# RMSNorm with every row written twice: two tiles' copies moved to VectorE as wide instructions, one copy and its store moved behind a row of the next tile

## The chip, the cores and the metric

The kernel runs on one core of one Trainium2 chip. The metric is the device time of one execution in microseconds (us), as the median of several runs. A ratio is the mean time of one kernel's runs over that of the other's in the same rounds, so it is not quite the ratio of the medians quoted. Beside each experiment the kernel before ran on the same chip; its medians there lie between 239.42 and 239.53 us.

## The reference

```python
def reference(x, gamma):                 # x: 8 x 512 x 2048 float32
    x_rep = np.repeat(x, 2, axis=1)      # every row twice
    rms = np.sqrt((x_rep ** 2).mean(axis=-1, keepdims=True) + 1e-6)
    return ((x_rep / rms) * gamma[None, None, :]).astype(np.float32)
```

33.6 MB are read and, as each row is written twice, 67.1 MB written.

## The kernel before

A tile is 512 rows: 4 rows (K) in each of 128 partitions. Its buffer has 8 row slots. A load fills slots 4 to 7; the scaled row k goes to slot 2k and a copy of it to slot 2k+1, so that a store writes 64 KB per partition in one piece. There are 8 tiles and 3 buffers. Cuts are marked with `# ...`.

```python
def store(i, k0, k1):
    nc.sync.dma_start(out=out_t[i, :, R * k0 * D : R * k1 * D],
                      in_=ys[i][:, R * k0 : R * k1, :].rearrange("p j d -> p (j d)"))
# ... square(i, k): ScalarE square with a row sum, then a root -> rms
# ... scale(i, k, rms): VectorE reciprocal, then row * rstd * gamma into slot 2k
def repeat(i, k0, k1, copy):
    y_r = ys[i].rearrange("p (k r) d -> p k r d", r=R)
    copy(out=y_r[:, k0:k1, 1, :], in_=y_r[:, k0:k1, 0, :])

def compute(i):
    for k in range(K):
        scale(i, k, square(i, k))
    repeat(i, 0, K // 2, nc.scalar.copy)            # first half: ScalarE
    repeat(i, K // 2, K, nc.vector.tensor_copy)     # second half: VectorE
# ... load(0), gamma, load(1), load(2)
loads_after = {2: (3, 4, 5), 4: (6, 7)}
for i in range(ntiles):
    compute(i)
    store(i, 0, K)
    for j in loads_after.get(i, ()):
        load(j, nc.sync)
```

All loads and stores are issued by SyncE, in program order. A load waits for the store that last used its buffer. In the queue the transfers stand as: loads 0, 1, 2, stores 0, 1, 2, loads 3, 4, 5, stores 3, 4, loads 6, 7, stores 5, 6, 7. There are five **turnovers**, places where loads give way to stores or stores to loads: in front of store 0, load 3, store 3, load 6 and store 5.

Of the kernel before, what the change touches and what calls it, by code (L numbers as in the profile page):

```python
# [1 line left out]

# [4 lines left out]


@with_exitstack
def kernel(  # L10
    ctx: ExitStack,
    tc: tile.TileContext,
    x: bass.AP,
    gamma: bass.AP,
    out: bass.AP,
):
    nc = tc.nc
    P = nc.NUM_PARTITIONS
    f32 = mybir.dt.float32
    Act = mybir.ActivationFunctionType  # L20
    Alu = mybir.AluOpType

    B, S, D = x.shape
    Bo, So, Do = out.shape
    R = So // S
    assert R == 2 and D == Do and B == Bo and So == S * R
    eps = 1e-6
    inv_d = 1.0 / float(D)


    K = 4
    N = B * S
    assert N % (P * K) == 0
    ntiles = N // (P * K)
    x_t = x.rearrange("b s d -> (b s) d").rearrange("(n p k) d -> n p k d", p=P, k=K)
    out_t = out.rearrange("b s d -> (b s) d").rearrange("(n p j) d -> n p (j d)", p=P, j=K * R)

    singles = ctx.enter_context(tc.tile_pool(name="singles", bufs=1))
    rows = ctx.enter_context(tc.tile_pool(name="rows", bufs=3))
    junk = ctx.enter_context(tc.tile_pool(name="junk", bufs=1, space=bass.MemoryType.PSUM))  # L40
    small = ctx.enter_context(tc.tile_pool(name="small", bufs=8))

    ys = []

    def load(i, eng, parts=1):


        y = rows.tile([P, K * R, D], f32, name="y")
        step = K // parts
        for k in range(0, K, step):  # L50
            at = K * (R - 1) + k
            eng.dma_start(out=y[:, at : at + step, :], in_=x_t[i, :, k : k + step, :])
        ys.append(y)

    def store(i, k0, k1):
        nc.sync.dma_start(  # L56
            out=out_t[i, :, R * k0 * D : R * k1 * D],
            in_=ys[i][:, R * k0 : R * k1, :].rearrange("p j d -> p (j d)"),
        )

    def square(i, k):
        sq = junk.tile([P, D], f32, name="sq")
        ss = small.tile([P, 1], f32, name="ss")
        nc.scalar.activation(  # L64
            out=sq[:], in_=ys[i][:, K * (R - 1) + k, :], func=Act.Square, accum_out=ss[:]
        )
        rms = small.tile([P, 1], f32, name="rms")
        nc.scalar.activation(out=rms[:], in_=ss[:], func=Act.Sqrt, scale=inv_d, bias=eps_t[:])  # L68
        return rms

    def scale(i, k, rms):
        rstd = small.tile([P, 1], f32, name="rstd")
        nc.vector.reciprocal(out=rstd[:], in_=rms[:])  # L73
        nc.vector.scalar_tensor_tensor(  # L74
            out=ys[i][:, R * k, :], in0=ys[i][:, K * (R - 1) + k, :], scalar=rstd[:], in1=gamma_b[:],
            op0=Alu.mult, op1=Alu.mult,
        )

    def repeat(i, k0, k1, copy):
        y_r = ys[i].rearrange("p (k r) d -> p k r d", r=R)  # L80
        copy(out=y_r[:, k0:k1, 1, :], in_=y_r[:, k0:k1, 0, :])  # L81

    def compute(i):
        for k in range(K):
            scale(i, k, square(i, k))
        repeat(i, 0, K // 2, nc.scalar.copy)
        repeat(i, K // 2, K, nc.vector.tensor_copy)


    ctx.enter_context(tc.manual_schedule())  # L90
    load(0, nc.sync, parts=2)
    gamma_b = singles.tile([P, D], f32, name="gamma_b")
    cuts = [0, *range(D // 4, D + 1, D // 8)]
    for c0, c1 in zip(cuts, cuts[1:]):
        nc.scalar.dma_start(out=gamma_b[0:1, c0:c1], in_=gamma[c0:c1].partition_broadcast(1))  # L95
    nc.gpsimd.partition_broadcast(out_ap=gamma_b[:], in_ap=gamma_b[0:1, :])  # L96
    eps_t = singles.tile([P, 1], f32, name="eps_t")
    nc.vector.memset(eps_t, eps)  # L98
    load(1, nc.sync)
    load(2, nc.sync)  # L100



    assert ntiles == 8
    loads_after = {2: (3, 4, 5), 4: (6, 7)}
    for i in range(ntiles):
        compute(i)
        store(i, 0, K)
        for j in loads_after.get(i, ()):
            load(j, nc.sync)  # L110


# [1 line left out]
_INS = ['x', 'gamma']  # L114
_OUTS = [((8, 1024, 2048), 'float32')]


# [23 lines left out]
```

## Time and profile before

| | before |
|---|---|
| median, 6 runs (lowest to highest) | 239.53 us (239.31 to 239.66) |
| VectorE, ScalarE busy | 96.5 and 101.0 us of 237.9 |
| share of the DMA engines' time that the one queue takes | 98.5% |
| rate from 2 to 235.5 us | 430 GB/s |
| stores 0, 3 and 5 issued at | 27.05, 115.86, 160.08 us |
| their first data at | 32.4, 119.4, 177.4 us |

The prediction below shows the lines.

### The profile page before, as it was taken

What the parts mean: (1) busy time and instruction counts of PE and PEld (TensorE: products, weight loads), DVE (VectorE), ACT (ScalarE), POOL (GpSimd) and SP (SyncE); (2) the same over time, 40 slices, a digit from 0 to 9 for tenths busy, and PEclk for the clock granted to TensorE, in tenths of its full rate; (3) what the DMA queues carried; (4) which work ended last, traced back from release to release, by engine and by line L of the source; (5) the groups of instructions that cost most, each with busy time, mean ns of one, the idle gap of its engine ahead of it and who ended that gap; (6) DMA issues with size and microseconds to landing.
All of it is one profiled execution on the core that took longest, in us unless ns stands there. A gap on an engine that the chain in (4) does not pass through costs nothing.

```text
span 237.9 us, 287 instructions
## 1 busy us (share of the span) xinstructions
DVE 96.5 (41%) x73; ACT 101.0 (42%) x106; POOL 2.5 (1%) x5
## 2 busy tenths in 40 slices
DVE  0049999960000000059999960000199990000000
ACT  2697999900000000099999920000599960000000
POOL 0030000000000000000000000000000000000000
DMA  7999998989899998999998999989998989999994
GB/s 265 436 446 441 441 441 353 530 353 496 386 452 430 397 485 353 441 441 441 441 518 364 464 419 430 452 369 430 435 518 364 518 364 485 397 452 430 408 474 176
DMA packets 2464, 100.69 MB, mean 423 GB/s; under 512 B 279, under 2 KB 285, under 8 KB 286
## 3 DMA queue, kind: packets, MB, share of 16 engines
q1 hardware_dynamic: 2448, 100.66, 98.5%
q14 instruction: 2, 0.02, 0.0%
q10 hardware_dynamic: 14, 0.01, 0.0%
HBM read 33.56 MB, written 67.11 MB: 423 GB/s over the span
## 4 chain that ended last, share of the span: by engine, by line
DMA 58%; ACT 12%; DVE 9%; issue 1%; POOLq 1%; ACTq 1%; SPq 0%
DMA y<-in_x_dram 33%; DMA out_dram<-y 21%; ACT sq L64 8%; DVE y L74 7%; DMA gamma_b<-in_gamma_dram 4%; ACT y L81 3%; DVE y L81 2%; ACT rms L68 1%; POOLq L136 1%; ACTq L95 1%; DVE rstd L73 0%; POOLq L96 0%; SPq L56 0%
## 5 line engine op out<-in xcount | busy, mean ns | idle before, releaser
L64 ACT ACTIVATE sq<-y 128x2048 f32<-128x2048 f32 x32 | 59.7, 1865 | 87.8 <-DMA y<-in_x_dram 87.8
L74 DVE SCALAR_TENSOR_TENSOR y<-y,rstd,gamma_b 128x2048 f32<-128x2048 f32 x32 | 75.3, 2352 | 4.1 <-POOL gamma_b L96 3.0
L73 DVE RECIPROCAL rstd<-rms 128x1 f32<-128x1 f32 x32 | 5.0, 158 | 94.6 <-ACT rms L68 94.3
L81 ACT COPY y<-y 128x4096 f32<-128x4096 f32 x8 | 28.7, 3590 | 1.4 <-DVE y L74 1.4
L81 DVE COPY y<-y 128x4096 f32<-128x4096 f32 x8 | 18.3, 2294 | 0.3
L68 ACT ACTIVATE rms<-ss,eps_t 128x1 f32<-128x1 f32 x32 | 9.4, 295 | 1.0
L64 ACT ACTIVATION_READ_ACCUMULATOR sq<-y 128x1 f32 x32 | 6.0, 187 | 0.0
L64 ACT ACT_TABLE_LOAD x1 | 1.3, 1283 | 3.0 <-issue 3.0
L96 POOL PARTITION_BROADCAST gamma_b<-gamma_b x1 | 2.3, 2294 | 12.2 <-DMA y<-in_x_dram 12.2
L68 ACT ACT_TABLE_LOAD x1 | 1.3, 1283 | 0.0
L98 DVE MEMSET eps_t<- 128x1 f32 x1 | 0.1, 59 | 0.8 <-PEq L125 0.8
L125 POOL MEMSET const-uint8-127<- 128x1 uint8 x1 | 0.1, 102 | 0.0
L125 POOL MEMSET const-bfloat16-1.0<- 128x1 bf16 x1 | 0.1, 101 | 0.0
L125 POOL MEMSET const-float32-0.0<- 128x1 f32 x1 | 0.1, 98 | 0.2 <-issue 0.2
L125 POOL MEMSET const-float32-1.0<- 128x1 f32 x1 | 0.1, 98 | 0.0
## 6 DMA issues: line engine op xcount, KB each, us to landing
y<-in_x_dram SPq DMA_DIRECT2D x7, 4096.0 KB, 14.6
y<-in_x_dram SPq DMA_DIRECT2D x2, 2048.0 KB, 7.4
out_dram<-y SPq DMA_DIRECT2D x8, 24.4
gamma_b<-in_gamma_dram ACTq DMA_DIRECT2D x6, 1.0 KB
gamma_b<-in_gamma_dram ACTq DMA_DIRECT2D x1, 2.0 KB
```

The source lines that it names most:

```text
L64: nc.scalar.activation(out=sq[:], in_=ys[i][:, K * (R - 1) + k, :], func=Act.Square, accum_out=ss[:])
L68: nc.scalar.activation(out=rms[:], in_=ss[:], func=Act.Sqrt, scale=inv_d, bias=eps_t[:])
L73: nc.vector.reciprocal(out=rstd[:], in_=rms[:])
L74: nc.vector.scalar_tensor_tensor(out=ys[i][:, R * k, :], in0=ys[i][:, K * (R - 1) + k, :], scalar=rstd[:], in1=gamma_b[:], op0=Alu.mult, o ...
L81: copy(out=y_r[:, k0:k1, 1, :], in_=y_r[:, k0:k1, 0, :])
L95: nc.scalar.dma_start(out=gamma_b[0:1, c0:c1], in_=gamma[c0:c1].partition_broadcast(1))
L96: nc.gpsimd.partition_broadcast(out_ap=gamma_b[:], in_ap=gamma_b[0:1, :])
L98: nc.vector.memset(eps_t, eps)
L125: nc = _bacc.Bacc("TRN2", target_bir_lowering=False, num_devices=1)
L136: with _tile.TileContext(nc) as tc:
```

## The change

In tiles 0 and 3 it frees ScalarE of its half of the copy; VectorE copies the whole tile there with one wide instruction. It also lets ScalarE start tile 6's first square before it copies tile 5's first half; store 5 must then wait for that copy.

```diff
     def compute(i):
         for k in range(K):
-            scale(i, k, square(i, k))
-        repeat(i, 0, K // 2, nc.scalar.copy)
-        repeat(i, K // 2, K, nc.vector.tensor_copy)
+            rms = square(i, k)
+            if i == 6 and k == 0:
+                repeat(5, 0, K // 2, nc.scalar.copy)
+                store(5, 0, K)
+            scale(i, k, rms)
+        if i in (0, 3):
+            repeat(i, 0, K, nc.vector.tensor_copy)
+        else:
+            if i != 5:
+                repeat(i, 0, K // 2, nc.scalar.copy)
+            repeat(i, K // 2, K, nc.vector.tensor_copy)
 ...
-        store(i, 0, K)
+        if i != 5:
+            store(i, 0, K)
```

## The prediction

> **What bounds the kernel now.** I began with the page: what each engine is busy with, then the strip of 40 slices and the table of DMA queues.
>
> ```profile
> DVE 96.5 (41%) x73; ACT 101.0 (42%) x106; POOL 2.5 (1%) x5
> ...
> DMA  7999998989899998999998999989998989999994
> ...
> q1 hardware_dynamic: 2448, 100.66, 98.5%
> ```
>
> VectorE and ScalarE work for two fifths of the span. The queue that SyncE issues on keeps the 16 DMA engines at 98.5% of the 237.9 us, and no inner slice falls below 8 tenths. Every load and store is on that queue. So I asked for the busy time of 2 to 235.5 us in one window, to see whether any hole is hidden by rounding.
>
> ```profile
> 2.00:235.50 233.50, 96.48 (x72) 101.02 (x106) 2.29 (x1) 1.00 1.00 430
> ```
>
> The last two columns are the DMA share and the rate: 1.00 and 430 GB/s. The bytes are fixed (33.56 MB read, 67.11 MB written), and 100.66 MB / 430 GB/s = 234.1 us; with about 1.7 us before the first packet and 2 us after the last that is the span. **The transfers are the bound.** A change of copies can matter only if it leaves the transfers without work for a while, or changes their order or size.
>
> So the question is how late each store may be issued. The chain of waits has the issues; its long DMA pieces are mostly waiting in line, since a store alone moves 8.39 MB, which at 430 GB/s is 19.5 us.
>
> ```profile
> 24.69 2.30 DVE y L81
> ...
> 27.05 25.77 DMA out_dram<-y
> 52.84 48.32 DMA y<-in_x_dram
> ...
> 115.86 24.36 DMA out_dram<-y
> 140.24 29.08 DMA y<-in_x_dram
> ```
>
> Read: store 0 is issued at 27.05 as soon as VectorE's copy ends, and lands 25.77 us later, not 19.5. Store 3 is issued at 115.86 and lands after 24.36. Each stood in line behind loads for some 5 us. To see when a store's own data begins I cut narrow windows around those moments. The window counts a packet at its start, and the packet records of the trace show 32 KB packets for loads and 64 KB for stores, one per partition. Columns: window, length, VectorE, ScalarE, GpSimd, clock, DMA share, GB/s.
>
> ```profile
> 31.00:32.30 1.30, 1.26 (x3) 1.27 (x4) 0.00 (x0) 1.00 0.00 0
> 32.30:32.60 0.30, 0.30 (x1) 0.30 (x1) 0.00 (x0) 1.00 3.02 1306
> ```
>
> ```profile
> 119.00:119.40 0.40, 0.40 (x1) 0.40 (x1) 0.00 (x0) 1.00 0.00 0
> 119.40:119.80 0.40, 0.40 (x1) 0.40 (x1) 0.00 (x0) 1.00 3.80 1638
> ```
>
> ```profile
> 177.30:177.80 0.50, 0.50 (x1) 0.50 (x1) 0.00 (x0) 1.00 2.00 852
> ```
>
> The zeros are no idle time: the last load packets are still moving. By the packet records the first 64 KB packets of store 0 start between 32.4 and 33.0 us, of store 3 between 119.4 and 120.1, of store 5 between 177.4 and 178.8, each directly behind the load in front of it. The **lead** (issue to first data) is 5.4 us for store 0 and 3.5 us for store 3. Store 5 is issued at 160.08, right behind load 7, and has 17.3 us. What lead is needed? The first load is issued at 0.72 us and its packets begin at 1.73 us, on the last engines by about 2.5: 1.0 to 1.8 us from an idle queue.
>
> **What the Trainium skill says.** "DMA: Bandwidth & Descriptors", section Queues, rings and completion order: on each DMA engine the descriptors of a queue are consumed in ring order. The trace agrees: the loads' packets finish before a store's begin at all three places. "HBM Reference", section Access, says that a core streaming alone reaches about 425 GB/s; the trace has 430. "VectorE: DVE Perf Modes", section The perf-mode tier table: an fp32 copy within SBUF runs at two elements a cycle (1227 ns for 2048). The trace's 128x4096 copy at 2294 ns agrees: 4096 / 2 / 0.96 GHz is 2133 ns, and the other 160 ns I take as a fixed cost of each instruction.
>
> **The change part by part.**
>
> ```profile
> L81 ACT COPY y<-y 128x4096 f32<-128x4096 f32 x8 | 28.7, 3590 | 1.4 <-DVE y L74 1.4
> L81 DVE COPY y<-y 128x4096 f32<-128x4096 f32 x8 | 18.3, 2294 | 0.3
> ```
>
> Tiles 0 and 3. Removed: two ScalarE copies, 2 x 3.59 = 7.2 us of an engine that is 42% busy. Widened: two VectorE copies from 128x4096 to 128x8192. I take the same two elements a cycle, as the pattern still has an even outer dimension (4 rows) and no overlap of source and destination: 8192 / 2 / 0.96 = 4267 ns, + 160 = 4.43 us, so **+2.13 us** on each.
> - Store 0: 27.05 + 2.13 = 29.18 us, lead 32.4 - 29.2 = 3.2 us. Needed 1.0 to 1.8. Hidden.
> - Store 3: 115.86 + 2.13 = 117.99, lead 119.4 - 118.0 = 1.4 us on the first engine and 2.1 on the last. Needed 1.0 to 1.8. Hidden, but this is the tight place: at worst some engines wait about 0.4 us.
>
> VectorE carries the 2.13 us into tiles 1, 2, 4 and 5, because it is nearly unbroken within a group. Store 1 would go from 39.2 to 41.3 us, store 2 from 51.39 to 53.5; they are wanted at 51.7 and 71.0, each a store (19.3 us) behind the one before. Store 4 goes from 128.25 to 130.4, wanted at 138.7. All have 8 us or more. Load 3, issued at 52.84 behind store 2, goes to about 53.9 and is wanted at 90. ScalarE starts tile 1 about a microsecond sooner; nothing waits for that.
>
> Tile 5 and 6. The copy of tile 5's first half (3.59 us) leaves 134.84 us and goes behind row 0's square of tile 6. Load 6 releases that square at 169.34, the root ends at 171.67, the copy ends near 171.6 + 3.6 = 175.2. So store 5 is issued at **175.2 instead of 160.08**, 15.1 us later. Lead: 177.4 - 175.2 = 2.2 us. Needed 1.0 to 1.8. Hidden. Its place in line is the same: loads 6 and 7 stood ahead of it already, and no other transfer overtakes.
> ScalarE's later squares of tile 6 move by 3.6 us, VectorE's by about 3.4 (its row 0 is not delayed). Store 6: 184.0 + 3.4 = 187.4, wanted at 196.7. Store 7: 196.4 + 3.4 = 199.8, wanted at 216.0. Hidden.
>
> Sum on the path: 0 + 0 + 0, with 0 to 0.4 us at store 3. Central 0.1 us: 239.63 + 0.1, called **239.7 us**.
>
> **The rivals.**
> - A store comes too late and the DMA engines run dry, at store 3 first. The lead left of 1.4 us is close to the 1.0 to 1.8 needed. If a store needs a lead of 2 us, the hole is 0.6 us there and nothing at store 5, so 240.2. If it needs 3 us, holes of 1.6 and 0.8 us: 242. Against it: I know no case of such need in this trace; the shortest lead it has is 3.5 us, and that left no hole.
> - The wide copy loses its fast mode. Then 8192 / 0.96 + 160 = 8.7 us, +6.4 over before: store 0 at 33.5 and store 3 at 122.2, holes of about 2.1 to 2.9 and 3.8 to 4.6 us, 246 us in all. Against it: the 4096 copy has the same kind of pattern, rows 4096 elements apart, and runs at the fast rate.
> - It gets faster. The last load packets before store 0 (starts 30.3 to 30.9) took about 2.1 us where 1.21 is the rule, on all engines: some 0.9 us lost, of unknown cause. If it comes from the moment of store 0's issue, the new moment may change it, so -0.9 to +0.9. Apart from that the transfers have no hole to close, and 2% (4.8 us) is not to be found.
> - VectorE becomes the bound: its sum goes to about 100.8 us of 238. It doesn't.
>
> **Range and chances.** The three runs of before lie within 0.15 us. The range takes the stretched packets away at its lower end (-0.7) and a hole of 1 us at its upper end: 238.9 to 240.6. Slower by 2% would need the lost fast mode, or several holes: 0.02. Faster by 2%: 0.01. Within: 0.97.
>
> **What the profile of the changed kernel would show.** Two VectorE copies of 128x8192 at 4.43 us and six of 128x4096; ScalarE's copies down to six. The store issues at 29.2, 118.0 and 175.2 us. The first data of stores 0, 3 and 5 still at 32.4, 119.4 and 177.4 (less 0.9 on all if the stretch vanishes), and a DMA share of 1.00 between 2 and 235.5 us. The prediction is wrong if store data begins visibly later than the end of the load in front of it, at store 3 above all, or if the order of transfers differs.

## The result and the profile after

| | before | after |
|---|---|---|
| median, 6 runs each | 239.53 us | 239.82 us |
| lowest to highest | 239.31 to 239.66 | 239.13 to 240.31 |
| ratio, 95% interval | | 1.0011 (0.9992 to 1.0029) |
| VectorE, ScalarE busy | 96.5, 101.0 us | 100.7, 94.3 us |

The time is the same. The page of the changed kernel (busy time by engine, the DMA strip, the queue), then its window from 2 to 235.5 us:

```profile
DVE 100.7 (42%) x73; ACT 94.3 (40%) x104; POOL 2.5 (1%) x5
...
DMA  7999999899998989999999989899999999898984
...
q1 hardware_dynamic: 2448, 100.66, 98.2%
```

```profile
2.00:235.50 233.50, 100.66 (x72) 94.34 (x104) 2.29 (x1) 1.00 1.00 430
```

4.2 us of work came to VectorE and 6.7 us left ScalarE, and the last two columns of the window are what they were: the DMA engines full, 430 GB/s. The groups of copies (busy us, mean ns of one, idle time in front):

```profile
L81 ACT COPY y<-y 128x4096 f32<-128x4096 f32 x6 | 21.6, 3594 | 5.2 <-DVE y L74 5.2
L81 DVE COPY y<-y 128x4096 f32<-128x4096 f32 (+1 forms) x8 | 22.6, 2826 | 0.3
```

ScalarE has six copies left. The second line's 2826 ns is a mean over two shapes. The timeline has the wide one by itself, in tiles 0 and 3, with SyncE's issues (SPq) behind it; the third piece has ScalarE's late copy of tile 5 and the issue of store 5. Columns: start, length, engine, line. A line with x2 or x3 takes several issues together: its start is that of the first, its length reaches to the end of the last.

```profile
24.48 4.43 DVE L81 COPY y<-y 128x8192 f32<-128x8192 f32 x1
...
28.93 12.56 SPq L56 DMA_DIRECT2D out_dram<-y  x2
```

```profile
113.01 4.43 DVE L81 COPY y<-y 128x8192 f32<-128x8192 f32 x1
...
117.47 0.34 SPq L56 DMA_DIRECT2D out_dram<-y  x1
```

```profile
171.31 3.59 ACT L81 COPY y<-y 128x4096 f32<-128x4096 f32 x1
...
174.92 25.06 SPq L56 DMA_DIRECT2D out_dram<-y  x3
```

So store 0 is issued 1.9 us later than before, store 3 1.6 and store 5 14.8. Did their data come later? The same narrow windows as in the prediction, of the changed kernel (last columns: DMA share, GB/s; packets are counted at their start):

```profile
31.00:31.50 0.50, 0.47 (x3) 0.47 (x3) 0.00 (x0) 1.00 0.00 0
31.50:32.30 0.80, 0.80 (x1) 0.18 (x1) 0.00 (x0) 1.00 3.04 1312
```

```profile
119.00:119.40 0.40, 0.40 (x1) 0.34 (x2) 0.00 (x0) 1.00 2.65 1147
...
177.30:177.80 0.50, 0.47 (x2) 0.50 (x1) 0.00 (x0) 1.00 3.89 1638
```

They came no later. 1312 GB/s over 0.8 us is 1.05 MB, the first 64 KB packet of store 0 on each of 16 engines; they start from 31.5 us on, where before it was 32.4. Store 3's start from 118.9 (before 119.4), store 5's from 177.3 (177.4). But store 0's data is 0.85 us *earlier*, although it was issued later, and at the end of the kernel nothing is left of that. The trace lists every DMA packet with its start, length and size. By these packet records of the two traces, this is what the last packet before each turnover took beyond the rule (1.213 us for a load's 32 KB, 2.418 for a store's 64 KB), as a mean over the 16 engines:

| us lost in front of | store 0 | load 3 | store 3 | load 6 | store 5 | sum |
|---|---|---|---|---|---|---|
| before | 0.87 | 0.00 | 0.03 | 0.02 | 0.04 | 0.96 |
| after | 0.10 | 0.35 | 0.00 | 0.24 | 0.15 | 0.84 |

The loss at the turnovers moved from one place to others. In the profiled run of the changed kernel one engine ran on to 237.33 us where the slowest of before stopped at 236.76: it lost 0.8 us in front of store 5, and up to 1.1 are lost on one engine in front of load 6.

### The profile page after: what moved, and what is told of

Its sections match the earlier page's. It is cut to its first block, busy times and chain, and to the rows that moved or that the text cites. A ratio compares the mean times of both kernels' runs of the same rounds, so it can differ in the third digit from the quotient of the medians.

```text
span 238.5 us, 285 instructions
## 1 busy us (share of the span) xinstructions
DVE 100.7 (42%) x73; ACT 94.3 (40%) x104; POOL 2.5 (1%) x5
## 3 DMA queue, kind: packets, MB, share of 16 engines
q1 hardware_dynamic: 2448, 100.66, 98.2%
## 4 chain that ended last, share of the span: by engine, by line
DMA 45%; DVE 22%; ACT 8%; issue 6%; POOLq 1%; ACTq 1%; SPq 0%
DMA y<-in_x_dram 32%; DVE y L74 19%; DMA out_dram<-y 9%; ACT sq L64 5%; DMA gamma_b<-in_gamma_dram 4%; ACT y L81 3%; DVE y L81 3%; POOLq L147 1%; DVE rstd L73 1%; ACTq L105 1%; ACT rms L68 1%; SPq L56 0%; POOLq L106 0%; SPq L52 0%
## 5 line engine op out<-in xcount | busy, mean ns | idle before, releaser
L81 ACT COPY y<-y 128x4096 f32<-128x4096 f32 x6 | 21.6, 3594 | 5.2 <-DVE y L74 5.2
L81 DVE COPY y<-y 128x4096 f32<-128x4096 f32 (+1 forms) x8 | 22.6, 2826 | 0.3
```

## The experiments

Two theories stand against each other. **Theory:** the DMA engines are the bound, each store has a lead from issue to first data, and a later issue costs nothing until the lead falls under what a transfer needs from issue to first data, and from there on one for one. **Rivals:** the two parts cost and gain and cancel; the queue makes good a late issue later on; the copies themselves are on the path. The diffs are against the changed kernel unless "before" is named.

### Each part alone

`a1_wide_only`: the wide copies, tile 5 as before.

```diff
-            if i == 6 and k == 0: ...copy and store of tile 5...
-            if i != 5:
-                repeat(i, 0, K // 2, nc.scalar.copy)
+            repeat(i, 0, K // 2, nc.scalar.copy)
 ...
-        if i != 5:
-            store(i, 0, K)
+        store(i, 0, K)
```

> Part one of the change alone: tiles 0 and 3 wide, tile 5 as before. My theory (the 16 DMA engines are the bound and each store has a lead left) expects the time of before, 239.6 us within 0.6, with stores 0 and 3 issued near 28.9 and 117.5 us and their data directly behind the load in front. Rival (two costs and gains of the two parts cancel in the whole change): this one alone is off by over 1 us, and the tile 5 part alone is off by as much the other way.

Measured: 239.81 us (239.51 to 241.42, 6 runs), ratio 1.0033 (1.0006 to 1.0061). Stores 0 and 3 issued at 28.93 and 117.47 us.

`a2_late5_only`: tile 5's copy and store moved, no wide copy.

```diff
-        if i in (0, 3):
-            repeat(i, 0, K, nc.vector.tensor_copy)
-        else:
+        if True:
```

> Part two of the change alone: tile 5's first half copied behind row 0 of tile 6, its store issued near 175 us instead of 160. Theory: 239.6 us within 0.6, because the store's data could not begin before 177.3 us in either case. Rival (cancelling parts): off by over 1 us against the first part.

Measured: 239.49 us (239.31 to 239.59), ratio 0.9998 (0.9986 to 1.0010). Store 5 was issued at 175.13 us and its data began at 177.36, as in the kernel before.

Both parts are worth nothing by themselves, so no cancelling is needed. The wide copies' 0.3% is barely clear of noise and comes from two of the six runs, above 241 us; the other four have a mean of 239.68. The two were not profiled, so what they had is not known. The section on turnovers takes up the profiled run (239.84 us).

### How late is too late

`b1_row1` and `b3_row3`: tile 5's copy behind row 1 or row 3 of tile 6 instead of row 0.

```diff
-            if i == 6 and k == 0:
+            if i == 6 and k == 1:      # b3_row3: k == 3
```

> The changed kernel, but tile 5's copy behind row 1's square of tile 6 (one square, accumulator read and root later, 2.22 us). Store 5 is then issued near 177.1 us. Theory: the store needs 1.0 to 1.8 us from issue to first data, so it begins at 178.2 to 178.9 where the load in front ended at 177.3 to 178.3: a hole of about 0.7 us on the engines that end last, 240.3 to 240.6 us in all, and 240 to 241 allowing for noise. Rival (the queue makes good a late issue, or the lead is not needed at all): 239.6 us, no hole. Rival (a store needs a lead of over 2.4 us): hole of 2 us or more, 241.5.

> The same copy behind row 3's square of tile 6: store 5 issued near 181.6 us, 6.7 us later than in the changed kernel. Theory: past the lead every microsecond counts in full, so the hole is about 6.7 - 1.4 = 5.3 us on the engines that end first and 5.0 on the last, and the time 244.6 us within 0.7. Rival (a later stretch makes it good, since store 6 and 7 have leads of 9 us and more): under 241 us.

Measured: 238.82 us (238.78 to 239.42; ratio 0.9976, 0.9963 to 0.9989) for row 1, 243.42 us (243.33 to 244.07; ratio 1.017) for row 3. The first is a miss, and not only in size: later was a little faster. The second came out 0.5 us under my range. SyncE's timeline of b1_row1, then that of b3_row3 and its windows (there is a hole when no packet starts for longer than one takes):

```profile
176.68 22.84 SPq L56 DMA_DIRECT2D out_dram<-y  x3
```

```profile
181.93 18.40 SPq L56 DMA_DIRECT2D out_dram<-y  x3
```

```profile
178.80:180.00 1.20, 1.17 (x3) 1.20 (x1) 0.00 (x0) 1.00 0.00 0
180.00:182.70 2.70, 2.67 (x2) 2.70 (x2) 0.00 (x0) 1.00 0.00 0
182.70:183.00 0.30, 0.30 (x1) 0.30 (x1) 0.00 (x0) 1.00 8.18 3495
```

The loads had ended by 178.74 us, the store is issued at 181.93, its first data starts at 182.77 on the first and 182.91 on the last engine (3495 GB/s x 0.3 us is one 64 KB packet on all 16). **So a store into an idle queue needed 0.84 to 0.98 us from issue to first data.** In b1_row1 store 5 is issued at 176.68 and starts at 177.52: the same 0.84. The last engine's load ended at 177.84, so the hole was on the early engines only (13 of 16), and those were not the ones that end last. Between the two profiled runs, 244.07 - 238.82 = 5.25 us, and store 5's data starts 5.07 to 5.25 us later: past the lead it counts in full, though stores 6 and 7 still had leads of 17 and 22 us. (The profiled run of b3_row3 was its slowest by 0.65 us; the medians differ by 4.60.)

`c1_t3_again` and `c4_t3_again`: the same at store 3, with one row, or all four, of tile 3 copied a second time.

```diff
             repeat(i, 0, K, nc.vector.tensor_copy)
+            if i == 3:
+                repeat(i, 0, 1, nc.vector.tensor_copy)      # c4_t3_again: 0, 4
```

> The changed kernel with one row of tile 3 (128x2048) copied a second time behind the wide copy, so that store 3 is issued 1.2 us later, near 118.7 us, while the load in front of it ends at 118.9 on the first DMA engine and 119.7 on the last. The two runs with store 5 held back showed 0.84 to 0.98 us from issue to first data. Theory (a store's hole counts only as far as it passes the engine that ends last): data at 119.5 to 119.7, no loss, 239.6 us within 0.6. Rival (the hole on the first engine counts): 0.7 us more, 240.4.

> The changed kernel with the whole wide copy of tile 3 done twice: store 3 issued 4.43 us later, near 121.9 us. Theory: data at 122.7 to 122.9, 3.1 us behind the engine that ends last, so 242.6 us within 0.7. It is also what the change would have cost there if the wide copy had run at one element a cycle. Rival (the place matters, since three tiles of work are behind it to make it good): under 240.5.

Measured: 240.60 us (240.49 to 240.77; ratio 1.0046) and 243.96 us (243.92 to 244.07; ratio 1.0185). Both are misses, by 0.4 and 0.7 us beyond my ranges. SyncE's timeline and the windows of c4_t3_again:

```profile
121.74 0.34 SPq L56 DMA_DIRECT2D out_dram<-y  x1
```

```profile
120.80:122.50 1.70, 1.67 (x3) 0.00 (x0) 0.00 (x0) 1.00 0.00 0
122.50:122.80 0.30, 0.30 (x1) 0.00 (x0) 0.00 (x0) 1.00 8.19 3495
```

Again 0.84 to 0.99 us from issue to data, at another place. Between the two kernels the time differs by 3.36 us and store 3's first data (119.16 in c1, 122.58 in c4) by 3.42. The hole itself is therefore as the theory has it. What both have on top came later: c1 has no hole in front of store 3 that the last engine feels (its loads end at 119.25, the store starts at 119.30), but the last packets in front of load 6 took 0.61 us too long and those in front of store 5 0.73. So c1's 240.60 us lies nearer to the 240.4 that I had given to the rival, a hole that counts on the first engine, than to my theory. What speaks against the rival is the trace, where the loss stands at other places, and b1_row1, where a hole on the early engines cost nothing. Whether c1's late store 3 brought the later losses about is not shown.

### Are the copies on the path at all?

`d_all_wide`: all tiles wide on VectorE, none on ScalarE (against before).

```diff
-        repeat(i, 0, K // 2, nc.scalar.copy)
-        repeat(i, K // 2, K, nc.vector.tensor_copy)
+        repeat(i, 0, K, nc.vector.tensor_copy)
```

> The kernel before with every tile's copy as one wide VectorE instruction and none on ScalarE. Theory: all stores keep a lead (store 0 and 3 as in the changed kernel, 4 near 131.8 us where 138.2 is wanted, 6 and 7 over 9 us), VectorE 112 us busy of 238, so 239.6 us within 0.6. Rival (VectorE, which gets all copies, becomes the bound of a stage): over 241.

Measured: 239.89 us (239.46 to 240.34), ratio 1.0014 (1.0001 to 1.0027). VectorE is busy for 113.3 us and ScalarE for 73.4, and the time is the same within 0.3%.

`e_no_copy` and its control `e2_copy_rows` (against before): each store becomes two of 8 KB rows. The first has no copies and reads slot 2k for both output rows; the control keeps the copies and reads slot 2k+1 for the odd rows.

```diff
-        nc.sync.dma_start(...one store of 64 KB per partition...)
+        for r in range(R):
+            nc.sync.dma_start(
+                out=out_t[i].rearrange("p (k r d) -> p k r d", r=R, d=D)[:, k0:k1, r, :],
+                in_=ys[i].rearrange("p (k r) d -> p k r d", r=R)[:, k0:k1, 0, :])   # control: r for 0
```

> The kernel before without any copy: each store is two of 4.19 MB, both reading the scaled rows, one writing the even and one the odd output rows. The result is right. Packets of 8 KB take the place of 64 KB. Theory: taking all 47 us of copies away gains nothing; the load packets show 0.611 us for 16 KB and 1.213 for 32 KB, so little cost per packet, and the time is 239.0 to 241. Rival (the copies are a cost): under 238.5.

> The control for the kernel without copies: the same two stores of 8 KB rows, but the copies of before kept and the odd rows read from them. Theory: the same time as without copies within 0.6 us. Rival: over 1 us longer than without copies.

Measured: 243.04 us (242.87 to 243.43) without copies and 242.77 (242.52 to 242.97) with them, ratios 1.0150 and 1.0141. The page of e_no_copy, then of e2_copy_rows (engines, queue):

```profile
DVE 78.4 (32%) x65; ACT 73.4 (30%) x98; POOL 2.5 (1%) x5
...
q1 hardware_dynamic: 9744, 100.66, 99.1%
```

```profile
DVE 96.5 (40%) x73; ACT 101.0 (42%) x106; POOL 2.5 (1%) x5
...
q1 hardware_dynamic: 9744, 100.66, 99.3%
```

45.7 us of engine work less (18.1 of VectorE, 27.6 of ScalarE), and not a microsecond of time. Both are slower than the kernel before, and e_no_copy lies 2.0 us above my range: the same bytes go in 9744 packets instead of 2448. By the packet records one of 8 KB takes 0.309 us, so eight take 54 ns more than one of 64 KB (2.418); for the 64 of those that each engine has, that is 3.5 us, about what is measured. With the packets alike, removing every copy gains nothing: that is the cleanest form of the answer.

### Why later was sometimes faster: the turnovers

In b1_row1 store 5 came just at the end of the load and the whole was faster. First theory: a store that waits in the queue stretches the last load packets in front of it, whatever the kernel. `f_row1_narrow` is a2_late5_only with row 1.

```diff
-            if i == 6 and k == 0:       # of a2_late5_only
+            if i == 6 and k == 1:
```

> The kernel before with only tile 5's copy moved, behind row 1 of tile 6 instead of row 0. The changed kernel in that form came out at 238.82 us, 0.24% under before, against my expectation. New theory: a store queued well ahead stretches the last load packets in front of it, and a store that comes just at their end does not; then the narrow form gains as well, 238.9 us within 0.3. Rival (the gain needs the wide copies too, or was chance): 239.5 us.

Measured: 239.48 us (239.35 to 239.62), ratio 0.9997. A miss by 0.3 us, where the rival had 239.5; the theory in that form fell. In the narrow kernel the packets in front of store 5 were not stretched to begin with (0.01 us with row 0, 0.00 with row 1), so there was nothing to win.

`h_wide_row1`: tiles all wide, except tile 5, whose copy is behind row 1 of tile 6.

```diff
-            if i == 6 and k == 0:
+            if i == 6 and k == 1:
-        if i in (0, 3):
+        if i != 5:
```

> The kernel with all copies wide (239.89 us; the last load packets in front of store 5 took 0.6 us too long on average) but tile 5's copy split as in the changed kernel and placed behind row 1 of tile 6, so that store 5 comes just at the end of the load. Theory (in the wide kernels a store queued ahead stretches the load in front of it, one just in time does not): 239.2 us within 0.3. Rival (the gain of that placing with two wide tiles was chance): 239.9 us.

Measured: 238.90 us (238.78 to 238.94), ratio 0.9979 (0.9966 to 0.9991), where all-wide had 239.89. (It differs from all-wide in tile 5's split copy too; b1_row1 differs from the changed kernel in the row alone.) So the gain with wide copies was no chance. The windows show what is odd in it. First a1_wide_only, where store 5 is issued at 159.38 us; then b1_row1, where it is issued 17 us later, at 176.68:

```profile
177.30:177.90 0.60, 0.60 (x1) 0.57 (x3) 0.00 (x0) 1.00 0.00 0
177.90:179.00 1.10, 1.06 (x3) 1.10 (x1) 0.00 (x0) 1.00 2.21 953
```

```profile
177.50:177.90 0.40, 0.00 (x0) 0.40 (x1) 0.00 (x0) 1.00 6.13 2621
```

The store that had waited in line all along starts its data between 177.97 and 178.93 us; the late one on all engines between 177.52 and 177.84 (2621 GB/s x 0.4 us is again 16 packets of 64 KB). In the first kernel the last load packets took 0.73 us too long on average, in the second 0.00.

`g_t0_again` puts the question at store 0: the kernel before with tile 0's second half copied twice by VectorE, so that store 0 is about as late as in the changed kernel (29.48 us against 28.93), with no wide instruction.

```diff
         repeat(i, K // 2, K, nc.vector.tensor_copy)
+        if i == 0:
+            repeat(i, K // 2, K, nc.vector.tensor_copy)
```

> The kernel before with tile 0's second half copied twice by VectorE, so that store 0 is issued near 29.2 us, as in the changed kernel, without any wide instruction. Theory: the last load packets in front of store 0 took 0.9 us too long on all engines in the three narrow kernels (store 0's data at 32.4 us) and hardly in the wide ones (31.5), and it is the moment of store 0's issue that decides; so data at 31.4 to 31.6 here, and part of it given back at later turnovers: 239.3 to 240.0 us. Rival (it is the wide instruction or ScalarE's missing copy): data still at 32.4, 239.5 us.

Measured: 239.15 us (239.10 to 239.49), ratio 0.9993 (0.9980 to 1.0005), 0.15 us under my range. SyncE's timeline and the window:

```profile
29.48 0.35 SPq L56 DMA_DIRECT2D out_dram<-y  x1
```

```profile
31.50:32.20 0.70, 0.67 (x3) 0.67 (x3) 0.00 (x0) 1.00 3.47 1498
```

Store 0's data starts at 31.53 us, not 32.4. So it does not take the wide instruction; the delay of store 0, and of VectorE's work behind it, is enough. The 0.87 us that were saved there were partly lost again in front of load 3 (0.19) and of store 3 (0.47).

| us lost in front of | store 0 | load 3 | store 3 | load 6 | store 5 | sum | median us |
|---|---|---|---|---|---|---|---|
| before | 0.87 | 0.00 | 0.03 | 0.02 | 0.04 | 0.96 | 239.53 |
| changed kernel | 0.10 | 0.35 | 0.00 | 0.24 | 0.15 | 0.84 | 239.82 |
| a2_late5_only | 0.92 | 0.00 | 0.01 | 0.00 | 0.01 | 0.94 | 239.49 |
| g_t0_again | 0.00 | 0.19 | 0.47 | 0.00 | 0.00 | 0.66 | 239.15 |
| b1_row1 | 0.07 | 0.35 | 0.00 | 0.12 | 0.00 | 0.54 | 238.82 |
| h_wide_row1 | 0.11 | 0.35 | 0.01 | 0.29 | 0.00 | 0.76 | 238.90 |
| d_all_wide | 0.13 | 0.23 | 0.00 | 0.10 | 0.60 | 1.06 | 239.89 |
| a1_wide_only | 0.12 | 0.29 | 0.00 | 0.29 | 0.73 | 1.43 | 239.81 |
| c1_t3_again | 0.02 | 0.25 | 0.00 | 0.61 | 0.73 | 1.61 | 240.60 |

Each row of losses is of one profiled run. The time follows the sum only roughly: a microsecond from the smallest to the largest, and 1.8 us of time. The changed kernel does not fit: it lost less than the kernel before and took 0.3 us longer. Its profiled run took 240.31 us; there the engines ended between 235.30 and 237.33 us, and a mean over them does not show the one that ended last. **What stays open** is why a turnover loses time in one kernel and not in another. A long wait in the queue alone is not it: store 5 waits 17 us in the kernel before and loses 0.04, and 18.6 us in a1_wide_only and loses 0.73. No run here tells which it is.

The best of these kernels beat the kernel before by 0.24%.

## Why the prediction was right

- **The bound** held. In e_no_copy 45.7 us of copies went away without gain, in d_all_wide they all went to one engine at a cost of 0.14% (0.01 to 0.27). One reading was off: the end of the span is 1.2 us behind the last data packet of the slowest engine (236.76 of 237.94), not 2. Nothing rests on it.
- **The wide copy** was put at 4.43 us and took 4.43. 4096 elements more took 2.13 us more, so it kept the rate of the narrow one, two a cycle at the prediction's 0.96 GHz; the rival of a lost fast mode fell. c4_t3_again, which holds VectorE for those 4.43 us once more, shows what that would have cost at store 3 alone: 243.96 us.
- **The issue times** were put at 29.18, 117.99 and 175.2 us and were 28.93, 117.47 and 174.92. Most of the difference is that the profiled run was ahead by 0.2 to 0.5 us at those places already.
- **The lead** was the step with the least ground: I took 1.0 to 1.8 us from the first load, in an empty machine. A store takes 0.84 to 0.99. So store 3, with 1.4 us, was safer than I said, and the 0 to 0.4 us set down there did not occur: in the changed kernel the packets in front of store 3 are not stretched and the store follows directly.
- **The stretched packets** in front of store 0 were named as the one unknown, with -0.9 to +0.9 us. The sign was left open; g_t0_again shows that delaying store 0 removes them. But the prediction had the 0.9 us vanish "on all" later times or not at all, and had no step by which they are lost again. First data came 0.85 us earlier at store 0, 0.53 at store 3 and 0.07 at store 5. That the total came within 0.1 us of 239.7 is therefore in part luck: a gain and losses at the turnovers, neither of them in the sum, nearly cancelled.
- **The rivals:** no store came too late, VectorE is at 42%. My sum of 0.1 us against measured 0.3 is inside the noise of both.

My expectations of single runs did worse than the prediction: b1_row1, b3_row3, c1_t3_again, c4_t3_again and f_row1_narrow came out 0.3 to 1.2 us outside the ranges I gave, g_t0_again 0.15 and e_no_copy 2.0. In e_no_copy it was the cost of the smaller packets; the others left the turnovers' own losses out, or put them in the wrong place.

## What to carry to other kernels

When the DMA engines are full, ask of each store not how long the work in front of it takes but how far its issue lies before its first data; as long as that stays above what an issue needs (about a microsecond here), work can be moved between engines for nothing (here from ScalarE to VectorE; the other direction was not tried). In b1_row1 a hole on the DMA engines that do not end last cost nothing; in b3_row3 and c4_t3_again a hole on all of them cost about one for one. Below half a per cent the losses at the turnovers decide here, and a sum of leads doesn't predict them.

## What the Trainium skill lacked or had wrong

- "DMA: Bandwidth & Descriptors", section Latency and other measured facts, gives about 600 ns to the first byte for a DMA issued from SyncE, and does not say from when it counts. From the start of the issue to the first packet it was 0.84 to 0.99 us for a store into an idle queue (b3_row3, c4_t3_again) and 1.01 us for the first load of the program. The issue itself is 0.34 us of that (c4_t3_again); counted from its end, the stores' 0.50 to 0.65 us agree with the page.
- No page that I read tells of the loss at a turnover between loads and stores on a full queue. Here the last packets before one took up to 1.1 us longer than their 1.213 or 2.418 us, on all engines in front of store 0 of the kernel before (0.87 on average), and the loss moved when a store was issued 2.4 us later (0.00 in g_t0_again).
- "DMA: Bandwidth & Descriptors" speaks of the cost of a packet for small ones; it has no measured cost for packets of 8 or 64 KB. Stores in 8 KB instead of 64 KB packets (9744 against 2448 in all) took 242.77 against 239.42 us: (9744 - 2448) / 16 = 456 more packets per engine in 3.35 us, an estimate of 7 ns each; the packet records give 54 / 7, about 8 ns.
- Not a lack: "HBM Reference", section Specifications (TRN2), is borne out: 430 GB/s from 2 to 235.5 us against its about 425 for a core that streams alone.
